# Delta heads: decay matrix and score matrix of a direction side by side in one buffer, both written by one multiply of 128x256

## The chip, the cores and the metric

One core of one Trainium2 chip runs the program. The metric is device time in microseconds (us). The kernel before takes 2635.76 us, the median of 3 runs (2635.53 to 2638.45).

## What is computed

One step of a backbone of two layers with shared code. A layer normalises its input (128 context tokens and 512 latent tokens, width 2048), makes one large input projection and hands its columns to three groups of heads: 8 gated delta heads, 4 attention heads and 4 pooling groups. Each result is multiplied by a gate of its own, all are concatenated and go through one output projection. The change lies in the delta heads:

```
def gated_delta_chunked(q, k, v, g, beta, s0):
    gc = jnp.cumsum(g, axis=-1)
    decay = jnp.exp(jnp.where(tri, gc[..., :, None] - gc[..., None, :], -jnp.inf))
    kb = k * beta[..., None]
    lmat = jnp.where(strict, jnp.einsum('nbhid,nbhjd->nbhij', kb, k) * decay, 0.0)
    rhs = jnp.concatenate([kb * jnp.exp(gc)[..., None], v * beta[..., None]], axis=-1)
    sol = lax.linalg.triangular_solve(lmat + eye, rhs, left_side=True, lower=True, unit_diagonal=True)
    w, u = sol[..., :DK], sol[..., DK:]
    attn = jnp.einsum('nbhid,nbhjd->nbhij', q, k) * decay
...
    def step(s, xs):
        v_new = u_i - jnp.einsum('bhcd,bhde->bhce', w_i, s)
        o = jnp.einsum('bhcd,bhde->bhce', qg_i, s) + jnp.einsum('bhij,bhje->bhie', attn_i, v_new)
        s = s * gl_i[..., None, None] + jnp.einsum('bhcd,bhce->bhde', kg_i, v_new)
```

It is run forwards and backwards over the tokens, with decays and betas of their own for each direction. What matters: `lmat` and `attn` are two products of the same keys (with keys and with queries), multiplied by the same decay matrix and by the same beta (the kernel puts the beta of `v_new` into `attn`).

## The kernel before, in words

**Order of the work.** The program is recorded as a list of operations in program order, and a planner (class `Sched`) then sets for each engine the order in which its instructions are issued. It simulates the program with a cost per instruction; whenever an engine is free it takes the ready operation that stands first in the program. A tile is given a place when its first operation is planned; a tag has a fixed number of places, and an operation whose tile finds none is put off until an older tile of the tag is dead. So the number and the lifetimes of the tiles of a tag decide the order on all engines. On the chip each engine issues its instructions in the planned order and waits by semaphores. All instructions are issued from one line, L499, so in the trace one tells them apart by tiles and shapes.

**Memory.** `memory()` lays the tags into regions: the slab S, the rounded slab R (operands of the large projections, `slabr` in the rows), and two regions W and V (`slabW`, `slabV`), each used for several things in turn. While the delta heads run, W holds four decay matrices `E` of 128x640 (two directions of two heads), two `qg` and `dj`; V holds four score matrices `At` of 128x640, two `ktok` and `cd`. The weights of the next layer's modulation, `ad2w`, lie over the start of W in two buffers.

**A head.** `delta(l, h, ins)` takes the transposed keys, queries and values of 5 chunks of 128 tokens. For each direction a row of cumulated decays is loaded from DRAM to all 128 partitions (a decay matrix, 320 KB), a mask is added, and five exponentials are taken. `to_tok` transposes the keys on TensorE. Then comes the score loop (L1234 to L1247): for a chunk, keys and queries are split into a rounded part and a rest, three products on TensorE give 128x256 in PSUM (keys by keys in the first 128 columns, keys by queries in the others), and four VectorE multiplies of 128x128 make `At` and then `E` of each direction, the latter in place.

After it the diagonal 32x32 blocks go through DRAM into 40 partitions, VectorE solves them in 31 steps of two instructions (`40xN` in the rows: a product and a sum), a `40x1024` copy transposes the result, and it goes back through DRAM. Block products on TensorE (32x32, then 64x64), which read `E`, build the inverse `XT`. Then comes the recurrence, 5 steps in both directions, whose products with `At` read the score matrix up to the last step. A normalisation of 128x5 instructions follows, the transposes, the multiplication into the gate tile `sza`, and the store of `sza`.

**What runs beside it.** `phase_a` calls `delta(h)` and then `head_in(h + 1)`, which makes the projections (products `psum<-slabr`) and convolutions of the next head, so the projections of head h+1 are the work that TensorE has beside head h. After the last head come four pooling groups:

```
        for h in range(H):
            self.delta(l, h, nxt)
            if h + 1 < H:
                nxt = self.head_in(l, h + 1)
        for g in range(4):
            self.pool_group(l, g)
            if l == 0:
                self.ada_cols(l + 1, 16 + 4 * g, 20 + 4 * g, "ad2w", "pr2", 2)
```

A pooling group has one projection for its input and one in `silu_gate`, for which it needs a place of `sza` (there are three) and banks of the PSUM tag `acc` (three); its output product is `psum<-slab,slabV` with 128x128 and 128x512. `ada_cols` loads `ad2w` and multiplies with it.

Of the kernel before, what the change touches and what calls it, by code (L numbers as in the profile page):

```python
# [13 lines left out]
ALU = mybir.AluOpType  # L14
# [9 lines left out]
NT = 5  # L24
# [19 lines left out]
WW = {"W": 4096, "V": 4480}  # L44
# [4 lines left out]
def toff(t):  # L49
    return 0 if t == 0 else 2 + 128 * t  # L50
# [451 lines left out]
class Body:  # L502
# [5 lines left out]
    def memory(self):  # L508
        tags = self.nc.tags

        def put(space, o, specs, top, rounded=False):
            for name, n, w in specs:
                self.nc.tag(name, space, w, [o + i * w for i in range(n)], rounded)
                o += n * w
            assert o <= top, (specs[-1], o, top)
            return o

        at = lambda name: tags[name].slots[0]
# [6 lines left out]
        put("V", 0, [("kpl", 1, 768), ("qps", 1, 640), ("qnh", 1, 640), ("qnl", 1, 640), ("knh", 1, 768), ("knl", 1, 768), ("wkl", 1, 256)], WW["V"], True)  # L525
        put("V", 0, [("cqh", 1, 1920), ("cql", 1, 1920)], WW["V"], True)
        put("W", 0, [("wrh", 1, 768), ("wrl", 1, 768), ("wqh", 2, 384), ("wql", 2, 384)], WW["W"], True)
        put("W", 0, [("E", 4, 640), ("qg", 2, 640), ("dj", 1, 128)], WW["W"])
        put("V", 0, [("At", 4, 640), ("ktok", 2, 640), ("cd", 1, 320)], WW["V"])
        put("W", at("E"), [("ad2w", 2, 2048)], WW["W"])  # L530
        put("V", at("cd"), [("wg", 1, 128)], WW["V"])
        fix = put("S", 0, [("cs", 1, 960), ("ones", 1, 128), ("cw", 1, 240), ("misc", 1, 20), ("dtb", 1, 32), ("nega", 1, 32),
                           ("bn", 1, 96), ("ccol", 1, 64), ("acl", 2, 32), ("bcl", 2, 32), ("mcol", 4, 32), ("raw", 2, 1024)]
# [4 lines left out]
        c = tags["q"].slots + tags["vT"].slots + tags["k"].slots  # L538
# [23 lines left out]
        t = self.nc.tag  # L562
# [620 lines left out]
    def delta(self, l, h, ins):  # L1183
        nc, a = self.nc, self.a
        v = nc.vector
        kT, qT, vT, sza = ins
        ident = self.ident
        E = []
        for d in range(2):
            e = self.T("E", [128, NT, 128])  # L1190
            nc.sync.dma_start(e.rearrange("p t c -> p (t c)"), self.gcd[0].rearrange("(d h t) c -> d h (t c)", d=2, h=8)[d, h].partition_broadcast(128))
            v.tensor_tensor(e, e, self.mask[d].unsqueeze(1).to_broadcast([128, NT, 128]), op=ALU.add)
            for t in range(NT):
                nc.scalar.activation(e[:, t], e[:, t], AF.Exp, bias=self.NGC[:, d * 8 + h, t:t + 1])
            E.append(e)
        ktok = self.T("ktok", [128, NT, 128])
# [3 lines left out]
        bneg, kgs = self.T("bneg", [128, 2, NT]), self.T("kgs", [128, 2, NT])  # L1200
# [29 lines left out]
        v.tensor_tensor(iz, rs, rs, op=ALU.mult)  # L1230
        v.scalar_tensor_tensor(bneg, iz.unsqueeze(1).to_broadcast([128, 2, NT]), -1.0, dh(self.BT), op0=ALU.mult, op1=ALU.mult)
        v.tensor_tensor(kgs, bneg, dh(self.EKG), op=ALU.mult)
        At = [self.T("At", [128, NT, 128]) for _ in range(2)]
        for t in range(NT):  # L1234
            p = self.ps("pr")
            o = toff(t)
            hi, lo = (self.T("kq", [128, 256], F32R) for _ in range(2))
            for i, x in enumerate((kT, qT)):
                c = slice(128 * i, 128 * i + 128)
                self.copy(hi[:, c], x[:, o:o + 128])  # L1240
                self.rest(lo[:, c], x[:, o:o + 128], hi[:, c])
            nc.tensor.matmul(p[:, 0:256], hi[:, 0:128], hi, start=True, stop=False)
            nc.tensor.matmul(p[:, 0:256], hi[:, 0:128], lo, start=False, stop=False)
            nc.tensor.matmul(p[:, 0:256], lo[:, 0:128], hi, start=False, stop=True)
            for d in range(2):
                v.scalar_tensor_tensor(At[d][:, t], p[:, 128:256], bneg[:, d, t:t + 1], E[d][:, t], op0=ALU.mult, op1=ALU.mult)
                v.scalar_tensor_tensor(E[d][:, t], p[:, 0:128], bneg[:, d, t:t + 1], E[d][:, t], op0=ALU.mult, op1=ALU.mult)  # L1247
        M = E
        cd = self.T("cd", [128, 10, 32])
        for b in range(4):  # L1250
# [29 lines left out]
        qg = []  # L1280
# [77 lines left out]
        for step in range(NT):  # L1358
            for d in range(2):
                t = 0 if step == 0 else (step if d == 0 else 5 - step)  # L1360
# [51 lines left out]
        for g0, g1 in ((0, 4), (4, 5)):  # L1412
            p = self.ps("o")
# [253 lines left out]
```

## Time and profile before

| what | value |
|---|---|
| time, median of 3 runs | 2635.76 us (2635.53 to 2638.45) |
| the profiled execution: time, span | 2642.71 us, 2640.6 us |
| mean granted clock of TensorE | 0.982 |
| ScalarE, GpSimd busy | 1026.8 us (39%), 739.7 us (28%) |
| moved over HBM | 313.07 MB read, 31.46 MB written |
| chain that ended last | TensorE 80%, DMA 6%, VectorE 3%, ScalarE 2%, GpSimd 1% |

PE is TensorE's matmuls, PEld its weight loads (which overlap the matmuls), DVE VectorE, ACT ScalarE, POOL GpSimd, SP the engine that issues the DMAs. Of two layers, the delta heads run from about 495 to 1060 us in the first and from about 1790 to 2350 us in the second. The granted clock is given as a share of full speed. Two levels occur, 1.2 and 2.4 GHz, so 0.50 is the lower one and a value between is a mean over a stretch.

### The profile page before, as it was taken

How to read it: one execution, taken by the hardware profiler on the slowest of the kernel's cores; microseconds unless marked ns; L12 is line 12 of the kernel's file. 1: busy time of each engine (PE TensorE's matmuls, PEld its weight loads, DVE VectorE, ACT ScalarE, POOL GpSimd, SP SyncE). 2: the span in 40 equal slices, each digit the busy share in tenths (PEclk: the TensorE clock that was granted, in tenths of full speed). 3: DMA queues.
4: the chain of work that ended last, by engine and by line, in shares of the span. 5: the costliest groups of instructions: out<-in, count | busy, mean ns of one | idle time of the engine just before them, and what ended most of it. 6: DMA issues, size and time to landing. Idle time of an engine off the chain costs nothing.

```text
span 2640.6 us, 52982 instructions
## 1 busy us (share of the span) xinstructions
PE 2541.0 (96%) x20553; PEld 2380.4 (90%) x20553; DVE 1664.4 (63%) x4229; ACT 1026.8 (39%) x2789; POOL 739.7 (28%) x825
## 2 busy tenths in 40 slices
PE   4999999999999999999988999999999999999998
PEld 1689999999999998878888999999999999988888
DVE  3545556888888886332257365678878887755225
ACT  3233345444444432222247333444444444323222
POOL 0021112354333333220025211233444333334002
PEclk7999999999999999999998999999999999999999
DMA  9944444332343333896755434523433334336225
GB/s 314 335 108 110 133 116 121 96 95 83 92 103 101 102 91 100 235 271 173 190 182 157 126 95 126 149 78 91 101 103 90 91 92 103 84 84 194 92 75 191
DMA packets 541202, 347.98 MB, mean 132 GB/s; under 512 B 103826, under 2 KB 499734, under 8 KB 540310
## 3 DMA queue, kind: packets, MB, share of 16 engines
q1 hardware_dynamic: 540950, 344.59, 46.7%
q8 instruction: 162, 2.65, 0.4%
q14 instruction: 90, 0.74, 0.1%
HBM read 313.07 MB, written 31.46 MB: 130 GB/s over the span
## 4 chain that ended last, share of the span: by engine, by line
PE 80%; DMA 6%; DVE 3%; ACT 2%; POOL 1%; issue 1%; SPq 1%; DVEq 0%; ACTq 0%
PE psum L499 80%; DVE slab L499 3%; DMA slab<-d 2%; DMA slab<-in_w_in_dram 1%; DMA slab<-in_w_ada_dram 1%; ACT slab L499 1%; POOL slabr L499 1%; DMA slabW<-in_w_ada_dram 1%; DMA d<-slab 1%; SPq L499 1%; ACT slabr L499 1%; ACT slabW L499 0%; DMA slab<-in_x_sample_dram 0%; DVE slabV L499 0%; DMA slabW<-d 0%
## 5 line engine op out<-in xcount | busy, mean ns | idle before, releaser
L499 PE MATMUL psum<-slabr 128*128 128x384 f32 (+2 forms) x11760 | 2011.1, 324 | 2.3 <-DVE slabW L499 1.0
L499 PEld LDWEIGHTS psum<-slabr 128*128 128x128 f32 x11760 | 1778.2, 190 | 86.9 <-issue 23.5
L499 POOL TENSOR_TENSOR slabr<-slab,slabr 128x512 fp32r<-128x512 f32 (+3 forms) x428 | 482.8, 1136 | 1200.3 <-ACT slabr L499 878.8
L499 ACT ACTIVATE slabr<-slab 128x512 fp32r<-128x512 f32 (+3 forms) x731 | 393.3, 548 | 879.2 <-PE psum L499 726.5
L499 DVE TENSOR_TENSOR slabr<-slab,slabr 128x512 fp32r<-128x512 f32 (+3 forms) x404 | 262.8, 654 | 416.1 <-ACT slabr L499 363.8
L499 PE MATMUL psum<-slab 128*128 128x128 f32 (+4 forms) x4375 | 434.7, 256 | 56.7 <-DVE slab L499 31.9
L499 DVE TENSOR_TENSOR slab<-slab 128x5 f32<-128x5 f32 (+20 forms) x1298 | 473.2, 376 | 19.2 <-DMA slab<-d 3.9
L499 ACT ACTIVATE slab<-psum 128x128 f32<-128x128 f32 (+6 forms) x823 | 276.1, 351 | 492.5 <-PE psum L499 384.7
L499 PEld LDWEIGHTS psum<-slab 128*128 128x128 f32 (+4 forms) x4375 | 352.1, 140 | 97.5 <-DVE slab L499 39.3
L499 DVE SCALAR_TENSOR_TENSOR slab<-slab 128x5 f32<-128x5 f32 (+7 forms) x618 | 348.2, 572 | 42.9 <-ACT slab L499 33.9
L499 ACT ACTIVATE slab<-slab 128x642 f32<-128x642 f32 (+4 forms) x240 | 141.1, 603 | 62.3 <-DVE slab L499 55.7
L499 DVE COPY slab<-psum 32x160 f32<-32x160 f32 (+9 forms) x214 | 84.0, 399 | 112.7 <-PE psum L499 98.0
L499 DVE TENSOR_SCALAR slab<-slab 128x1 f32<-128x1 f32 (+7 forms) x363 | 111.4, 326 | 29.0 <-ACT slabW L499 16.2
L499 POOL TENSOR_SCALAR slab<-slabV,slab 128x128 f32<-128x128 f32 x128 | 58.1, 460 | 217.5 <-PE psum L499 216.9
L499 DVE SCALAR_TENSOR_TENSOR slab<-psum,slab 128x128 f32<-128x128 f32 (+1 forms) x216 | 80.1, 378 | 56.4 <-PE psum L499 54.5
L499 DVE TENSOR_REDUCE slab<-psum 128x4 f32<-128x16 f32 (+3 forms) x104 | 39.5, 380 | 106.5 <-PE psum L499 105.3
L499 PE MATMUL psum<-slab,slabW 32*32 32x32 f32 (+2 forms) x1216 | 80.8, 219 | 14.5 <-DMA slab<-d 7.8
L499 POOL TENSOR_TENSOR slab<-slab 128x640 f32<-128x640 f32 (+5 forms) x46 | 68.1, 1481 | 95.1 <-ACT slab L499 77.8
L499 ACT ACTIVATE slab<-psum,slab 128x256 f32<-128x256 f32 (+2 forms) x93 | 58.7, 641 | 78.3 <-DVE slab L499 74.6
L499 PEld LDWEIGHTS psum<-slab,slabW 32*32 32x32 f32 (+2 forms) x1216 | 66.3, 132 | 23.1 <-DMA slab<-d 10.7
L499 DVE SCALAR_TENSOR_TENSOR slab<-slab,psum 128x128 f32<-128x128 f32 (+2 forms) x160 | 62.0, 395 | 37.2 <-PE psum L499 25.9
L499 PE MATMUL psum<-slab,slabV 128*128 128x128 f32 (+1 forms) x352 | 72.4, 296 | 1.9 <-DVE slab L499 1.4
(61 smaller groups left out, 1384.5 us busy)
## 6 DMA issues: line engine op xcount, KB each, us to landing
slab<-in_w_in_dram SPq DMA_DIRECT2D x186, 512.0 KB
slab<-in_w_ada_dram SPq DMA_DIRECT2D x32, 1024.0 KB
slabW<-in_w_ada_dram SPq DMA_DIRECT2D x32, 1024.0 KB
slab<-in_w_out_dram SPq DMA_DIRECT2D x64, 512.0 KB
slabW<-d SPq DMA_DIRECT2D x64, 320.0 KB
slabV<-in_w_ada_dram SPq DMA_DIRECT2D x32, 512.0 KB
slabW<-in_w_ada_dram SPq DMA_DIRECT2D x32, 512.0 KB
d<-slab SPq DMA_DIRECT2D x32, 320.0 KB
```

The costliest lines, as they stand in the source:

```text
L499: op.inst = getattr(getattr(nc, op.eng), op.meth)(*[real(x) for x in op.a], **{n: real(x) for n, x in op.k.items()})
```

## The change

A direction's decay matrix and score matrix now lie in one buffer of 128 x 5 x 2 x 128, `EA0` in W for the forward direction and `EA1` in V for the backward one, two buffers each. For each chunk the score matrix has the first 128 columns and the decay matrix the next. Queries and keys change places in the split, so that PSUM holds the products in the same order, and one multiply of 128x256, with the decay matrix read twice, writes both. The reload of a decay matrix writes 5 runs of 128 elements per partition instead of one of 640. `ad2w` lies over `EA0`.

```diff
--- before.py
+++ after.py
@@ -525,9 +525,9 @@
         put("V", 0, [("kpl", 1, 768), ("qps", 1, 640), ("qnh", 1, 640), ("qnl", 1, 640), ("knh", 1, 768), ("knl", 1, 768), ("wkl", 1, 256)], WW["V"], True)
         put("V", 0, [("cqh", 1, 1920), ("cql", 1, 1920)], WW["V"], True)
         put("W", 0, [("wrh", 1, 768), ("wrl", 1, 768), ("wqh", 2, 384), ("wql", 2, 384)], WW["W"], True)
-        put("W", 0, [("E", 4, 640), ("qg", 2, 640), ("dj", 1, 128)], WW["W"])
-        put("V", 0, [("At", 4, 640), ("ktok", 2, 640), ("cd", 1, 320)], WW["V"])
-        put("W", at("E"), [("ad2w", 2, 2048)], WW["W"])
+        put("W", 0, [("EA0", 2, 1280), ("qg", 2, 640), ("dj", 1, 128)], WW["W"])
+        put("V", 0, [("EA1", 2, 1280), ("ktok", 2, 640), ("cd", 1, 320)], WW["V"])
+        put("W", at("EA0"), [("ad2w", 2, 2048)], WW["W"])
         put("V", at("cd"), [("wg", 1, 128)], WW["V"])
         fix = put("S", 0, [("cs", 1, 960), ("ones", 1, 128), ("cw", 1, 240), ("misc", 1, 20), ("dtb", 1, 32), ("nega", 1, 32),
                            ("bn", 1, 96), ("ccol", 1, 64), ("acl", 2, 32), ("bcl", 2, 32), ("mcol", 4, 32), ("raw", 2, 1024)]
@@ -1185,10 +1185,13 @@
         v = nc.vector
         kT, qT, vT, sza = ins
         ident = self.ident
-        E = []
+        E, At, EA = [], [], []
         for d in range(2):
-            e = self.T("E", [128, NT, 128])
-            nc.sync.dma_start(e.rearrange("p t c -> p (t c)"), self.gcd[0].rearrange("(d h t) c -> d h (t c)", d=2, h=8)[d, h].partition_broadcast(128))
+            ea = self.T(f"EA{d}", [128, NT, 2, 128])
+            At.append(ea[:, :, 0])
+            e = ea[:, :, 1]
+            EA.append(ea)
+            nc.sync.dma_start(e, self.gcd[0].rearrange("(d h t) c -> d h t c", d=2, h=8)[d, h].partition_broadcast(128))
             v.tensor_tensor(e, e, self.mask[d].unsqueeze(1).to_broadcast([128, NT, 128]), op=ALU.add)
             for t in range(NT):
                 nc.scalar.activation(e[:, t], e[:, t], AF.Exp, bias=self.NGC[:, d * 8 + h, t:t + 1])
@@ -1230,21 +1233,19 @@
         v.tensor_tensor(iz, rs, rs, op=ALU.mult)
         v.scalar_tensor_tensor(bneg, iz.unsqueeze(1).to_broadcast([128, 2, NT]), -1.0, dh(self.BT), op0=ALU.mult, op1=ALU.mult)
         v.tensor_tensor(kgs, bneg, dh(self.EKG), op=ALU.mult)
-        At = [self.T("At", [128, NT, 128]) for _ in range(2)]
         for t in range(NT):
             p = self.ps("pr")
             o = toff(t)
             hi, lo = (self.T("kq", [128, 256], F32R) for _ in range(2))
-            for i, x in enumerate((kT, qT)):
+            for i, x in enumerate((qT, kT)):
                 c = slice(128 * i, 128 * i + 128)
                 self.copy(hi[:, c], x[:, o:o + 128])
                 self.rest(lo[:, c], x[:, o:o + 128], hi[:, c])
-            nc.tensor.matmul(p[:, 0:256], hi[:, 0:128], hi, start=True, stop=False)
-            nc.tensor.matmul(p[:, 0:256], hi[:, 0:128], lo, start=False, stop=False)
-            nc.tensor.matmul(p[:, 0:256], lo[:, 0:128], hi, start=False, stop=True)
+            nc.tensor.matmul(p[:, 0:256], hi[:, 128:256], hi, start=True, stop=False)
+            nc.tensor.matmul(p[:, 0:256], hi[:, 128:256], lo, start=False, stop=False)
+            nc.tensor.matmul(p[:, 0:256], lo[:, 128:256], hi, start=False, stop=True)
             for d in range(2):
-                v.scalar_tensor_tensor(At[d][:, t], p[:, 128:256], bneg[:, d, t:t + 1], E[d][:, t], op0=ALU.mult, op1=ALU.mult)
-                v.scalar_tensor_tensor(E[d][:, t], p[:, 0:128], bneg[:, d, t:t + 1], E[d][:, t], op0=ALU.mult, op1=ALU.mult)
+                v.scalar_tensor_tensor(EA[d][:, t], p[:, 0:256].rearrange("p (i c) -> p i c", i=2), bneg[:, d, t:t + 1], E[d][:, t].unsqueeze(1).to_broadcast([128, 2, 128]), op0=ALU.mult, op1=ALU.mult)
         M = E
         cd = self.T("cd", [128, 10, 32])
         for b in range(4):
```

The planner makes a new order from it. Three places are shown.

TensorE, at the end of the heads of layer 0 (`slabr` is an operand of a projection; `slabW` and `slabV` are the regions W and V; `slab` is everything else; 128x512 with `slabV` is a pooling product). Before:

```order
L499 MATMUL psum<-slabr 128x384 x7
L499 MATMUL psum<-slab,slabV_3862 128x128
L499 MATMUL psum<-slabr 128x384 x28
L499 MATMUL psum<-slab,slabV_3862 128x512
L499 MATMUL psum<-slab 128x128 x4
L499 MATMUL psum<-slab,slabV_3862 128x128
L499 MATMUL psum<-slab 128x128
L499 MATMUL psum<-slab,slabW_3582 128x128
L499 MATMUL psum<-slabr 128x256 x5
L499 MATMUL psum<-slab,slabV_3862 128x512
L499 MATMUL psum<-slabr 128x256 x31
```

Now, the end of a run of 19 rows that hold no projection:

```order
L499 MATMUL psum<-slab,slabW_3582 128x128 x2
L499 MATMUL psum<-slab 128x128
L499 MATMUL psum<-slab,slabV_3587 128x128
L499 MATMUL psum<-slab 128x128
L499 MATMUL psum<-slab,slabW_3582 128x128
L499 MATMUL psum<-slab 128x128 x4
L499 MATMUL psum<-slab,slabW_3582 128x128 x2
L499 MATMUL psum<-slab,slabV_3587 128x128
L499 MATMUL psum<-slab 128x128 x5
L499 MATMUL psum<-slab,slabV_3587 128x128
L499 MATMUL psum<-slab,slabV_3587 128x512
L499 MATMUL psum<-slab,slabW_3582 32x32 x10
```

Before, the first pooling product is followed by head 6's four transposes and then by projections; now it stands behind the recurrence of head 6 and is followed at once by the first block products of head 7.

VectorE, the same place (`40xN` are steps of head 7's inverse, `128x5` the normalisation of head 6, `slab<-psum,slab 128x128` and `slab<-slab,psum 128x128` its recurrence). Before:

```order
L499 COPY slab<-psum 128x512
L499 TENSOR_TENSOR slab<-slab 40x192
L499 SCALAR_TENSOR_TENSOR slab<-slab 128x5
L499 TENSOR_TENSOR slab<-slab 40x8x24
L499 TENSOR_SCALAR slab<-slab 128x5
L499 TENSOR_TENSOR slab<-slab 40x175
L499 TENSOR_SCALAR slab<-slab 128x5
L499 TENSOR_TENSOR slab<-slab 40x7x25
```

Now:

```order
L499 SCALAR_TENSOR_TENSOR slab<-slab,psum 128x128 x2
L499 TENSOR_TENSOR slab<-slab 40x175
L499 TENSOR_TENSOR slab<-slab 40x7x25
L499 TENSOR_TENSOR slab<-slab 40x156
L499 SCALAR_TENSOR_TENSOR slab<-psum,slab 128x128
L499 TENSOR_TENSOR slab<-slab 40x6x26
L499 SCALAR_TENSOR_TENSOR slab<-psum,slab 128x128
L499 TENSOR_TENSOR slab<-slab 40x135
```

At the same step of head 7's inverse, head 6 was in its normalisation and is now in its recurrence.

SP, the DMAs around the reload of head 2 in layer 0 (`d_1398` holds the cumulated decays and their exponentials; `out_dram` 128x128 are head 0's final states; a load of `d_4839` or `d_4824` into 40x1024 is the way into the inverse of head 1). Before:

```order
L499 DMA d_4839<-slabV_3862 128x10x32
L499 DMA slabW_3582<-d_1398 128x640
L499 DMA slab<-in_w_in_dram 128x8x128
L499 DMA slabW_3582<-d_1398 128x640
L499 DMA slab<-d_4839 40x1024
L499 DMA out_dram<-slab 128x128 x2
L499 DMA slab<-in_w_in_dram 128x8x128 x2
L499 DMA slab<-in_state_delta_fwd_dram 128x128
L499 DMA slab<-in_state_delta_bwd_dram 128x128
L499 DMA slabW_3582<-d_1398 128x640 x2
```

Now:

```order
L499 DMA d_4824<-slabV_3587 128x10x32
L499 DMA slab<-d_4824 40x1024
L499 DMA slab<-in_w_in_dram 128x8x128
L499 DMA out_dram<-slab 128x128 x2
L499 DMA slab<-in_w_in_dram 128x8x128 x2
L499 DMA slabW_3582<-d_1398 128x640
L499 DMA slab<-in_state_delta_fwd_dram 128x128
L499 DMA slab<-in_state_delta_bwd_dram 128x128
L499 DMA slabW_3582<-d_1398 128x5x128
L499 DMA slabW_3582<-d_1398 128x640
L499 DMA slabV_3587<-d_1398 128x5x128
```

The two decay matrices of head 2 (now 128x5x128) stood ahead of the inverse's load and of head 0's outputs, and now stand behind them and behind three loads of projection weights.

## Rows read from the trace of the kernel before

**Rows 1.** The page, part 1: busy us, share of the span, instructions.

```profile
PE 2541.0 (96%) x20553; PEld 2380.4 (90%) x20553; DVE 1664.4 (63%) x4229; ACT 1026.8 (39%) x2789; POOL 739.7 (28%) x825
```

**Rows 2.** Windows: length, then busy PE, PEld, DVE, ACT, POOL, clock, DMA share, GB/s.

```profile
528.00:1023.00 495.00, 488.24 (x4120) 479.06 (x4119) 405.65 (x1077) 216.76 (x665) 197.48 (x221) 1.00 0.37 94
1821.00:2277.00 456.00, 450.18 (x3731) 442.79 (x3730) 375.87 (x994) 205.76 (x635) 185.99 (x205) 0.99 0.36 95
```

**Rows 3.** Waits of PE, 495 to 1023 us: total us, times, longest.

```profile
PE psum L499 <- DVE slabW L499: 0.5, 1, 0.5
```

**Rows 4.** Timeline, 1031 to 1058 us: start, length, instruction; idle before and releaser bracketed.

```profile
1031.40 1.02 PE L499 MATMUL psum<-slab,slabV 128*128 128x512 f32 x2
...
1034.03 0.70 PE L499 MATMUL psum<-slab 128*128 128x128 f32 x4 [1.61 <-DVE slab L499]
...
1036.57 1.03 DVE L499 COPY slab<-slab 40x1024 f32<-40x1024 f32 x1
...
1037.45 0.76 ACT L499 ACTIVATE slab<-psum 128x384 f32<-128x384 f32 x2 [3.10 <-DMA d<-slab]
...
1038.58 1.43 PE L499 MATMUL psum<-slabr 128*128 128x256 f32 x5
...
1045.92 0.73 PE L499 MATMUL psum<-slab,slabW 32*32 32x32 f32 x40
...
1046.57 1.49 PE L499 MATMUL psum<-slabr 128*128 128x384 f32 x7
...
1049.50 2.17 PE L499 MATMUL psum<-slabr 128*128 128x384 f32 x14
...
1051.61 1.20 PE L499 MATMUL psum<-slab,slabW 64*64 64x64 f32 x20
```

**Rows 5.** Windows at the end of the heads, columns as in group 2.

```profile
1036.00:1038.00 2.00, 0.64 (x2) 0.35 (x3) 1.70 (x6) 0.55 (x2) 0.00 (x0) 0.50 0.63 209
1030.00:1042.00 12.00, 8.24 (x31) 5.43 (x30) 9.05 (x36) 1.46 (x4) 0.94 (x4) 0.73 0.35 98
2327.00:2339.00 12.00, 8.41 (x31) 5.72 (x30) 8.58 (x34) 1.46 (x4) 0.28 (x4) 0.74 0.35 99
```

**Rows 6.** VectorE's groups by form: count, busy us, mean ns, idle before, releaser.

```profile
L499 DVE SCALAR_TENSOR_TENSOR slab<-psum,slab 128x128 f32<-128x128 f32 x192 | 62.2, 331 | 39.9 <-PE psum L499 38.0
L499 DVE SCALAR_TENSOR_TENSOR slabV<-psum,slab,slabW 128x128 f32<-128x128 f32 x160 | 49.2, 340 | 4.6 <-PE psum L499 4.6
L499 DVE SCALAR_TENSOR_TENSOR slabW<-psum,slab,slabW 128x128 f32<-128x128 f32 x160 | 48.7, 338 | 0.0
...
L499 DVE TENSOR_TENSOR slab<-slab 40x220 f32<-40x220 f32 x64 | 27.6, 431 | 0.6
...
L499 DVE COPY slab<-slab 40x1024 f32<-40x1024 f32 x16 | 22.0, 1375 | 0.1
...
L499 DVE TENSOR_TENSOR slab<-slab 40x135 f32<-40x135 f32 x64 | 18.6, 290 | 1.0
...
L499 DVE SCALAR_TENSOR_TENSOR slab<-slab,psum 128x384 f32<-128x384 f32 x32 | 17.5, 548 | 9.0 <-ACT slab L499 8.8
...
L499 DVE SCALAR_TENSOR_TENSOR slab<-slab,psum 128x256 f32<-128x256 f32 x32 | 13.1, 410 | 0.9 <-ACT slab L499 0.9
```

**Rows 7.** Chain that ended last: start us, length us, what.

```profile
597.02 4.17 DMA slabW<-d
...
745.09 4.31 DMA slab<-in_w_in_dram
```

**Rows 8.** Timeline of PE in layer 1's recurrence, columns as in group 4.

```profile
2365.54 0.38 PE L499 MATMUL psum<-slab 128*128 128x128 f32 x2
2365.76 0.39 PE L499 MATMUL psum<-slab,slabV 128*128 128x128 f32 x2
```

**Rows 9.** Waits of PE, 1060 to 1200 us, columns as in group 3.

```profile
PE psum L499 <- DMA slabW<-in_w_ada_dram: 4.6, 4, 2.3
```

**Rows 10.** Chain at the end of layer 0's heads.

```profile
1023.81 12.30 DVE slab L499 x37
```

## The prediction

> **What bounds the kernel now.** I read the page first: TensorE is busy for 96% of the span and VectorE for 63% [rows 1]. A share over the whole span says nothing about the stage that is changed, so next come the two stretches in which the heads follow each other, one per layer: there TensorE is busy for 488.24 of 495 us and for 450.18 of 456 us, at a granted clock of 1.00 and 0.99, with VectorE busy for 82% of both [rows 2]. So 12.6 us of idle TensorE are all that a faster head could win there, and the list of waits gives 0.5 us of the first stretch to VectorE's writes into W, where half of the changed multiplies go [rows 3]. The score stage of a head is hidden by the projections of the next one.
>
> The cover ends once per layer, at the end of the heads. There the projections of the pooling groups are the only other work, and the third group stops half way: its second PSUM bank stays taken until an older gate is read out, which waits for a gate tile that is free only once head 6 is stored. The rows show that: after the pooling product at 1031.40 TensorE waits for VectorE, ScalarE's gate evacuation at 1037.45 waits 3.10 us for the store, and the projections go on at 1038.58 [rows 4]. The granted clock is 0.50 (1.2 GHz) at 1036 to 1038 us, behind these microseconds with little work [rows 5]. In the 12 us around it TensorE has 8.24 us of busy time and a mean clock of 0.73, and the same in layer 1 [rows 5]. That is the stretch to watch.
>
> **The change, part by part.**
>
> *The multiply.* 320 instructions of 128x128, at 340 and 338 ns, become 160 of 128x256 [rows 6]. No row has this very form; the nearest are an instruction of 128x256 at 410 ns and one of 128x384 at 548 ns, each with one operand in PSUM [rows 6]. I take 440 ns, just above the row of the same size, because here one operand is read twice. VectorE goes from 97.9 us to 160 x 0.44 = 70.4 us, 27.5 us less (by the bounds 32 to 10 us less). On the path that sets the end: nothing, since TensorE waits 0.5 us for these writes in a whole stretch [rows 3]; if that cover were gone, 1.7 us per head. The 256 columns are the same three products with q and k exchanged: nothing.
>
> *The strided reload.* A decay matrix was loaded in runs of 2560 B, and now in runs of 512 B. The projection weights already arrive in runs of 512 B, 512 KB in 4.31 us, where a decay matrix of 320 KB took 4.17 us [rows 7]. So the load stays near 4 us: bounds 0 and 0.3 us, taken as 0. The mask, the exponentials and the block copies read rows 256 apart instead of 128, with the same runs of 128: 0.
>
> *Where the buffers live and when they come free.* A decay matrix was free after the last block product with it, before its head's recurrence. Now it shares a buffer with the score matrix, which the last step of the recurrence still reads. Two buffers per direction stay, so head h+2 can reload only after head h has ended. The SyncE rows show it: the reload of head 2 stands behind the outputs of head 0 and three projection loads instead of ahead of them. What hides this is the distance to the multiply: in the steady stretch a reload of 4.2 us, a mask and ten exponentials fit beside the previous head. I price it at 0 on TensorE. If that cover is gone it is one reload per head on the head's own chain, which TensorE sees only where it has no projections left.
>
> *The order at the end of the heads.* This is where the sum is made. In the order before, head 6 ends its recurrence under the projections, and what lies bare is its normalisation between the inverse of head 7. In the changed order head 6 is later, and the projections run out in the middle of its recurrence: 19 rows of TensorE, from the third step to the pooling product, have no projection among them. The bare stretch now has three pieces.
>
> 1. The rest of the recurrence, on VectorE between the inverse of head 7: 19 steps of the inverse, whose groups lie between 290 and 431 ns (mean about 0.355: 6.7 us), 8 of its other multiplies at 0.33 (2.6 us) and the copy at 1.4 us [rows 6], together 10.7 us. TensorE has 20 products in it at 0.22 us each, from start to start [rows 8], 4.4 us. Dry: 6.3 us.
> 2. From the end of that copy to the first block product of head 7, which waits for the inverse to go to DRAM and back: 1037.60 to 1045.92, 8.3 us, in the trace [rows 4]. There projections cover it; now TensorE has 12 products of 0.22 us and one 128x512 of 1.0 us [rows 4], 3.6 us. Dry: 4.7 us, less the two multiplies that still follow the copy (0.7 us): 4.0 us.
> 3. The block products of head 7 up to the first 64x64 ones: 1045.92 to 1052.81, 6.9 us, in the trace, with 21 projections (3.7 us) among them [rows 4]. Bare I take 5 us with the other 3.2 us of work. Dry: 1.8 us.
>
> Together 12.1 us dry per layer. The stretch that it replaces has between 3.8 us (12 minus 8.24 us of products) and 6.6 us (12 minus 5.43 us of weight loads) [rows 5]; I take 6.6, since a lone product's busy time holds its own latency. So +5.5 us per layer. The bounds are +8.3, with 3.8 us, and 0, if pieces 2 and 3 lie inside piece 1 and nothing but its 6.3 us is dry. The clock took 12 x 0.27 = 3.2 us per layer before [rows 5]. The new stretch is twice as long but a little over half filled: its clock costs at least the same, and at most 4 us more, if all of its 11 us of work (4.4, 3.6 and 3.2) ran at half speed and so took 11 us longer, of which the 12 us dry hide most. I take the same.
>
> *The gate weights of layer 1.* Their two buffers lie over the decay buffers in W, so in layer 0 the first load now waits for the end of head 7 instead of its block products, about 100 products later. TensorE already waits 4.6 us for these loads [rows 9]. Bounds 0 and twice that; since the first is then used 36 products after its issue instead of 40, I take 0.
>
> **Sum.** 2 x 5.5 = +11 us on the profiled execution, 2642.7 to 2653.7 us. That execution lies 6.95 us above the median of the runs (2642.71 against 2635.76), so in terms of the median: 2646.8, say 2646 us, 0.4% slower. A measurement of this kernel can tell about 0.2% from no change, 5.3 us.
>
> **The rivals.**
>
> *Faster: the shorter multiply arrives.* Each head's chain is about 1.7 us shorter, and if head 6 gets through its recurrence before the projections run out, the bare stretch shrinks: its present price is 6.6 + 3.2 us per layer. Four tenths of that gone in both layers give 2635.8 - 8 = 2628 us. It decides from the point where head 6 is some 5 us earlier than the changed order has it. Against it: VectorE also has the inverse of head 7 between, and the reload now waits for head 4. The Trainium skill (VectorE: DVE Perf Modes, Rules for kernel authors) tells authors to minimise the number of VectorE instructions, and would expect this side; the trace agrees on the instruction (410 ns for twice the columns), not yet on the span. Chance 0.13.
>
> *No change: the two ends cancel.* In the new order the normalisation of head 6 no longer has the inverse between its small steps, which took 1023.81 to 1036.1 us [rows 10]; if pieces 2 and 3 overlap with it better than I reckon, the new stretch is about as dry as the old one: 2636 us. Chance 0.22.
>
> *Slower still.* The half filled stretch drops to 1.2 GHz early (+4 us per layer) and the gate weights wait twice as long (+4.6 us): 2646 + 12.6 = 2659 us. The rows have the clock at 0.50 after a few microseconds with little work [rows 5]. The Trainium skill (TensorE: Matmul & The Clock Gate, Why this matters for your kernels) warns that idle gaps between matmul bursts throw the engine back to its lower clock; the trace agrees, at 0.50 here. Chance 0.18.
>
> That the change does not do what it says would be a multiply of 128x256 as slow as two of 128x128, 678 ns; the row of 128x384 at 548 ns rules it out [rows 6].
>
> **How the numbers follow.** The forecast, 2641 to 2652 us, has 0.47, and with the slower rival 0.65 lie above 2641. No change has 0.22, faster 0.13. The range goes from 2635, which takes in most of no change, to 2660, with the slower rival; left out are the faster side and what lies above, about 0.2.
>
> **What would show it.** VectorE busy 25 to 30 us less; a group of 160 multiplies of 128x256 near 440 ns; the stretches where the heads follow each other as full as now; at the end of the heads a bare stretch of some 23 us in place of 7, with TensorE waiting for VectorE and for the loads from DRAM, and a granted clock under 1 for at least as long. I am wrong if TensorE's idle time there does not grow, if the steady stretches open gaps at the mask (a late reload), or if the time moves with VectorE's.

## The result, and the profile after

The changed kernel takes 2660.97 us, the median of 4 runs (2659.87 to 2662.72), beside 2635.65 us of the kernel before: a ratio of 1.0094 with an interval of 1.0077 to 1.0112. It is 25 us slower, more than twice the 11 us of the forecast, and a microsecond above the range.

The page, part 1 of the changed kernel (busy us, share of the span, instructions), answers to [rows 1]. TensorE has as many instructions as before, and is busy 11.6 us longer.

```profile
span 2659.7 us, 52763 instructions
PE 2552.6 (96%) x20553; PEld 2387.0 (90%) x20553; DVE 1650.1 (62%) x4054; ACT 1017.0 (38%) x2792; POOL 756.9 (28%) x837
```

VectorE's groups by form: the wide multiply has two groups, one per region. It takes 474 ns on average where the two that it replaces took 678 [rows 6]: 75.8 us in place of 97.9, so 22.1 us less.

```profile
L499 DVE SCALAR_TENSOR_TENSOR slabW<-psum,slab,slabW 128x256 f32<-128x256 f32 x80 | 38.1, 477 | 11.6 <-PE psum L499 11.3
L499 DVE SCALAR_TENSOR_TENSOR slabV<-psum,slab,slabV 128x256 f32<-128x256 f32 x80 | 37.7, 471 | 0.0
```

VectorE as a whole is busy only 14.3 us less, where 25 to 30 were forecast. The planner sets more than the order: for some operations it also chooses the engine, and in the new plan 12 instructions of 128x642 that ScalarE had (94 before, 82 now) are VectorE's. First before, then after:

```profile
L499 DVE TENSOR_SCALAR slab<-slab 128x642 f32<-128x642 f32 x2 | 1.1, 548 | 0.0
L499 DVE TENSOR_SCALAR slab<-slab 128x642 f32<-128x642 f32 x14 | 12.9, 921 | 5.3 <-ACT slab L499 5.0
```

Windows over the stretches in which the heads follow each other (columns as in group 2). They are fuller than before [rows 2]: 2.8 us of TensorE idle in 472, 3.5 in 469. The loss is not here.

```profile
528.00:1000.00 472.00, 469.18 (x3874) 461.57 (x3872) 378.20 (x941) 207.16 (x651) 206.06 (x216) 1.00 0.38 97
1821.00:2290.00 469.00, 465.46 (x3856) 457.49 (x3855) 372.19 (x940) 206.60 (x653) 201.82 (x214) 0.99 0.36 94
```

It is at the end of the heads. The timeline of TensorE there, layer 0:

```profile
1023.96 0.95 PE L499 MATMUL psum<-slabr 128*128 128x384 f32 x4
...
1033.35 1.22 PE L499 MATMUL psum<-slab 128*128 128x128 f32 x5 [1.01 <-DVE slab L499]
...
1038.81 0.48 PE L499 MATMUL psum<-slab 128*128 128x128 f32 x1 [2.90 <-ACT slabW L499]
...
1040.98 2.08 PE L499 MATMUL psum<-slab,slabV 128*128 128x512 f32 x2 [0.44 <-DVE slab L499]
1043.15 0.59 PE L499 MATMUL psum<-slab,slabW 32*32 32x32 f32 x14
...
1050.19 1.01 PE L499 MATMUL psum<-slab,slabW 64*64 64x64 f32 x7
...
1054.30 0.78 PE L499 MATMUL psum<-slabr 128*128 128x256 f32 x2
```

The last projection (`slabr`) starts at about 1024.6 us and the next at 1054.30. Before, the last one started at 1031.2 and the next at 1038.58 [rows 4], 7.4 us later. I call the time from the start of one projection to the start of the next the **bare stretch**: 29.7 us now, and 30.7 us in layer 1. Windows over the two, same columns: the granted clock is 0.73 and 0.71.

```profile
1024.60:1054.30 29.70, 21.95 (x193) 15.66 (x192) 18.93 (x64) 7.86 (x35) 9.61 (x17) 0.73 0.28 78
2329.60:2360.30 30.70, 21.75 (x193) 15.67 (x192) 21.15 (x64) 7.80 (x35) 9.62 (x17) 0.71 0.27 76
```

The 128x512 product (two records) took 2.08 us there, at a granted clock of 0.50, and 1.02 us before [rows 4]. The waits of TensorE in the first of these stretches:

```profile
PE psum L499 <- DVE slab L499: 3.8, 7, 1.0
PE psum L499 <- ACT slabW L499: 3.4, 2, 2.9
PE psum L499 <- ACT slab L499: 0.3, 1, 0.3
```

### The profile page after: what moved, and what is told of

The parts are those of the page before. It is cut to its first block, busy times and chain, and to the rows that moved or that the text cites. A ratio compares the mean times of both kernels' runs of the same rounds, so it can differ in the third digit from the quotient of the medians.

```text
span 2659.7 us, 52763 instructions
## 1 busy us (share of the span) xinstructions
PE 2552.6 (96%) x20553; PEld 2387.0 (90%) x20553; DVE 1650.1 (62%) x4054; ACT 1017.0 (38%) x2792; POOL 756.9 (28%) x837
## 4 chain that ended last, share of the span: by engine, by line
PE 78%; DMA 8%; DVE 5%; ACT 1%; SPq 1%; issue 1%; POOL 0%; DVEq 0%; ACTq 0%
PE psum L499 78%; DVE slab L499 5%; DMA slab<-d 2%; DMA slabW<-in_w_ada_dram 2%; DMA slab<-in_w_ada_dram 1%; DMA slab<-in_w_in_dram 1%; DMA d<-slab 1%; SPq L499 1%; ACT slab L499 1%; DMA slabV<-d 0%; DVE slabV L499 0%; ACT slabW L499 0%; POOL slabr L499 0%; DMA slab<-in_x_sample_dram 0%; ACT slabr L499 0%
## 5 line engine op out<-in xcount | busy, mean ns | idle before, releaser
L499 PE MATMUL psum<-slabr 128*128 128x256 f32 (+2 forms) x11760 | 1998.8, 323 | 0.9 <-ACT slabr L499 0.9
L499 POOL TENSOR_TENSOR slabr<-slab,slabr 128x512 fp32r<-128x512 f32 (+3 forms) x440 | 496.1, 1136 | 1245.2 <-ACT slabr L499 954.1
L499 ACT ACTIVATE slab<-psum 128x128 f32<-128x128 f32 (+7 forms) x823 | 276.5, 352 | 601.8 <-PE psum L499 502.1
L499 DVE TENSOR_TENSOR slab<-slab 128x5 f32<-128x5 f32 (+21 forms) x1298 | 475.7, 376 | 35.6 <-DMA slab<-d 12.2
L499 DVE SCALAR_TENSOR_TENSOR slab<-slab 128x5 f32<-128x5 f32 (+8 forms) x618 | 345.4, 570 | 47.7 <-ACT slab L499 42.7
L499 ACT ACTIVATE slab<-slab 128x642 f32<-128x642 f32 (+4 forms) x228 | 132.3, 596 | 54.5 <-DVE slab L499 49.5
L499 DVE TENSOR_SCALAR slab<-slab 128x1 f32<-128x1 f32 (+8 forms) x375 | 125.9, 355 | 33.8 <-ACT slabW L499 15.3
L499 PE MATMUL psum<-slab,slabW 128*128 128x128 f32 (+2 forms) x896 | 101.8, 242 | 10.8 <-DMA slab<-d 9.8
L499 PEld LDWEIGHTS psum<-slab,slabW 128*128 128x128 f32 (+2 forms) x896 | 82.8, 156 | 23.8 <-DMA slab<-d 14.2
L499 PE MATMUL psum<-slab,slabV 32*32 32x32 f32 (+3 forms) x672 | 69.9, 245 | 3.3 <-DVE slab L499 2.4
```

The source lines that it names most:

```text
L499: op.inst = getattr(getattr(nc, op.eng), op.meth)(*[real(x) for x in op.a], **{n: real(x) for n, x in op.k.items()})
```

## The experiments

Every ratio is against the kernel before, run beside it, whose median was 2636.42 us for the first four runs, 2640.74 for the next four, and 2639.61 for the last four. Three theories stood at first. **L**: the longer lifetime of the decay matrix makes the bare stretch. **S**: the strided loads or the shared buffer cost. **M**: the wide multiply costs. Each kernel has a plan of its own, of order and engines, unless the text says otherwise.

**1. The decay matrices held, nothing else.** The kernel before; in the planner's books the last product with `At` also holds `E`.

```diff
-                    nc.tensor.matmul(pt, At[d][:, t], Zt, start=False, stop=(nmm == 14))
+                    last = nc.tensor.matmul(pt, At[d][:, t], Zt, start=False, stop=(nmm == 14))
+                    if step == NT - 1:
+                        E[d].t.left += 1
+                        E[d].t.ops.append(last)
+                        last.tiles.append(E[d].t)
```

> Theory L (lifetimes): the loss comes from the decay matrix being held until the last step of its head's recurrence; head h+2 starts later, the projections run out inside head 6's recurrence, and the bare stretch that follows runs at the lower clock. Then holding the decay matrices of the kernel before, with its separate buffers, contiguous loads and four 128x128 multiplies, loses most of it: 2650 to 2662 us, and a stretch of 15 to 20 us at 1.2 GHz at the end of the heads in both layers. Theory S (strided access): the loads in runs of 512 B and the wider buffer cost; this kernel has neither: 2636 us. Theory M (the wide multiply or the order that follows from its length): 2636 us too.

Measured: 2649.73 us, ratio 1.0054 (1.0040 to 1.0067). In this plan the longer lifetime costs 13 to 14 us, a little over half of the loss, with no strided load and no wide multiply. The bare stretch is 12.8 us in both layers; the clock is at 1.2 GHz for 10.2 us in each, less than the 15 to 20 forecast.

**2. Merged buffers, two multiplies.** The change, with the multiply written as two of 128x128.

```diff
-                v.scalar_tensor_tensor(EA[d][:, t], p[:, 0:256].rearrange("p (i c) -> p i c", i=2), ...
+                v.scalar_tensor_tensor(At[d][:, t], p[:, 0:128], bneg[:, d, t:t + 1], E[d][:, t], ...
+                v.scalar_tensor_tensor(E[d][:, t], p[:, 128:256], bneg[:, d, t:t + 1], E[d][:, t], ...
```

> The merged buffers with two 128x128 multiplies per direction and chunk. Theory L: as the kernel with held decay matrices, within 3 us, 2650 to 2662 us, with VectorE busy some 25 us more than with the one multiply. Theory S: slower than the held kernel by what the change cost, so 2655 to 2661 us beside 2636 there. Theory M: back to 2636 us, since the wide multiply is gone.

Measured: 2647.02 us, 1.0044 (1.0031 to 1.0057), and 12.8 and 12.7 us bare. As the held kernel: S falls, and the strided loads cost nothing that can be measured between these two plans. But theory L explains only half, and the other half goes with the multiply or with the plan made for it.

**3. One multiply, lifetimes apart.** `E` and `At` of a direction are tiles of their own with places 640 columns apart, and the multiply writes across both.

```diff
-        put("W", 0, [("EA0", 2, 1280), ("qg", 2, 640), ("dj", 1, 128)], WW["W"])
-        put("V", 0, [("EA1", 2, 1280), ("ktok", 2, 640), ("cd", 1, 320)], WW["V"])
+        for i, sp in enumerate("WV"):
+            self.nc.tag(f"At{i}", sp, 640, [0, 1280])
+            self.nc.tag(f"E{i}", sp, 640, [640, 1920])
...
-                v.scalar_tensor_tensor(EA[d][:, t], p[:, 0:256].rearrange("p (i c) -> p i c", i=2), ...
+                v.scalar_tensor_tensor(Pair(At[d], E[d], t), p[:, 0:256].rearrange("p (i c) -> p i c", i=2), ...
```

> The one multiply of 128x256 is kept, but decay matrix and score matrix are tiles of their own that lie 640 columns apart, so the decay matrix is free after the last block product and is reloaded contiguously. Theory L: the loss is gone, 2628 to 2638 us, and the stretch at 1.2 GHz at the end of the heads is back to 7 us or less. Theory S: gone as well, 2630 to 2638 us. Theory M: the loss stays, 2655 to 2661 us.

Measured: 2641.17 us, 1.0016 (1.0006 to 1.0026). M falls: the wide multiply is there and most of the loss is gone. The bare stretch is 6.6 us, shorter than before, yet the kernel is not faster than before.

**4. The kernel before, once more.**

> The kernel before once more, for a second profile. The profiled execution of before took 2642.7 us, 7 us above the median of the runs; its trace has three drops of the clock in the stretches where the heads follow each other. If those drops differ from execution to execution, this one shows others or none and takes 2635 to 2643 us with the same 7 us of lower clock at the end of the heads.

Measured: 2641.08 us in one run. Drops of the clock in the steady stretches do differ from execution to execution: this profile has one at 2125 us, where the first had 1.00, and none at 681 and 2203 us, where the first had them. Two executions of one kernel so differ by some microseconds, and a term is better read from stretches than from spans. At the end of the heads the bare stretch is 7.2 and 7.3 us again, with the clock at 1.2 GHz for 6.8 and 3.4 us.

Now theory **O** was added: the other half comes from the plan that the planner makes when it reckons with the shorter multiply. Runs 5 to 7 put each kind of multiply into each order.

**5. The change beside them.** No edit.

> The change itself, beside the other kernels of this call on one chip. It measured 25 us over the kernel before, while the held kernel and the one with merged buffers and two multiplies lose only 11 to 13 us. All theories: 2655 to 2663 us here too; if it comes out near 2648 us instead, half of the loss belonged to the earlier occasion and not to the kernel.

Measured: 2661.67 us, 1.0087 (1.0073 to 1.0101), bare stretches of 30.2 and 29.9 us. The loss belongs to the kernel.

**6. The order of the change, two multiplies issued.** When the order has been made, each wide multiply is issued as its two halves.

```diff
-            op.inst = getattr(getattr(nc, op.eng), op.meth)(*[real(x) for x in op.a], ...
+            for a, k in op.halves:
+                op.inst = getattr(getattr(nc, op.eng), op.meth)(*[real(x) for x in a], ...
```

> The order of the change, instruction by instruction on every engine, but each wide multiply is issued as two of 128x128 at its place. Theory O (the second half of the loss comes from the order that the planner makes with the shorter multiply, in which head 6 is later still): as the change, 2655 to 2663 us. Theory M (the wide multiply itself costs): back to the kernel with two multiplies, 2645 to 2650 us.

Measured: 2673.5 us, 1.0135 (1.0116 to 1.0153): 12 us slower than the change, where neither theory had it. In this order the wide multiply is a gain. The bare stretch is 30.0 and 30.1 us, as in run 5, so the 12 us lie elsewhere. In the profile (the slowest of the four runs) TensorE is idle for 6.1 and 8.1 us where the heads follow each other, against 3.4 and 4.3 us in run 5, most of it in waits for the loads of the inverse. The clock is at 1.2 GHz there for 6.8 and 17 us, and in run 5 not at all; such falls vary between executions. Windows of run 6, then of run 5, columns as in group 2:

```profile
528.00:1000.00 472.00, 465.93 (x3821) 456.03 (x3820) 389.98 (x1001) 205.39 (x646) 202.99 (x216) 0.99 0.37 94
1821.00:2290.00 469.00, 460.90 (x3866) 449.84 (x3867) 377.57 (x965) 204.60 (x648) 196.68 (x207) 0.98 0.37 94
```

```profile
528.00:1000.00 472.00, 468.60 (x3871) 461.00 (x3871) 378.93 (x943) 207.93 (x653) 205.17 (x217) 1.00 0.37 96
1821.00:2290.00 469.00, 464.68 (x3868) 456.56 (x3866) 376.84 (x945) 207.35 (x655) 202.64 (x215) 1.00 0.37 94
```

**7. The order of run 2, one multiply issued.** The same edit the other way: the first half issues nothing, the second the wide multiply.

> The order of the kernel with merged buffers and two multiplies, but each pair is issued as one multiply of 128x256 at the place of the second. Theory O: as that kernel or a little less, 2643 to 2649 us. Theory M: as the change, 2655 to 2663 us.

Measured: 2647.1 us, 1.0026 (1.0014 to 1.0038), bare stretch 12.8 us twice. With runs 2 (1.0044), 5 and 6 this makes a square: with either multiply the order of the change is the slower one, by 0.6 to 0.9% of the time, and in either order the wide multiply is no loss (in the older order its intervals overlap with those of two). M is out. O stands, though the 12 us of run 6 were not in its forecast.

**8. Added products in the gaps.** 40 products of 128x128 per layer that nothing reads, planned only where TensorE has nothing else.

```diff
+        if h == H - 1:
+            with nc.later(1000000):
+                for _ in range(40):
+                    op = nc.tensor.matmul(p1[:, 384:512], ident, ident, start=True, stop=True)
...
```

> The change with 40 added products of 128x128 (the identity by itself, into an unused quarter of a PSUM bank) in the gaps of TensorE at the end of the heads of each layer; nothing reads them. Theory C (most of the loss at the end of the heads is TensorE running at 1.2 GHz after the half filled stretch): the stretch at the lower clock shrinks from 17 and 20 us to 7 or less, and the time falls by 8 to 15 us, to 2646 to 2653 us. Theory W (the loss is waiting alone, and work done at the lower clock lies inside the waits): the clock stays up but the time does not fall by more than 3 us, 2657 to 2662 us.

Measured: 2662.23 us, 1.0090 (1.0077 to 1.0103). It told nothing apart: the clock still fell, to 0.50 for 14 and 17 us, only later, when the block products came. The bare stretch is 27.5 and 29.1 us, with TensorE idle for 2.3 and 2.9 us of it. Run 12 adds products further on.

**9. The change with one number altered.** The planner's cost of the wide multiply.

```diff
+        if meth == "scalar_tensor_tensor" and onps and n == 256 and len(a[0].shape) == 3:
+            return 0.36
```

> The change with one number altered: the planner reckons 0.36 us for the wide multiply instead of 0.40. Every instruction is the same, the merged buffers and their lifetimes too; only the order on the engines differs, and the longest run of products without a projection falls from 101 (recurrence of head 6 to block products of head 7) to 59. Theory O (the order at the end of the heads decides): 10 to 20 us less than the change, 2640 to 2652 us. Theory B (the merged buffer costs by itself, whatever the order): within 5 us of the change, 2656 to 2666 us.

Measured: 2647.58 us, 1.0031 (1.0020 to 1.0043), bare stretches of 14.1 and 15.0 us. The same operations in the same merged buffers, and 14 us less. The expectation has every instruction the same, which is not quite so: the planner also chose other engines for some, and the 12 of 128x642 are ScalarE's again. B falls, and O is shown on the change itself, if the plan is taken as a whole, with order and engines.

**10. The same for run 3**, with `return 0.47`.

> The kernel with one multiply and lifetimes apart (2641 us), with the planner reckoning 0.47 us for the multiply, which is what it took on the chip (473 ns), instead of 0.40. Theory O: with no long run of products without projections (34 at most) and earlier heads it is at or below the kernel before, 2625 to 2638 us. If the truer number does not help: 2640 to 2648 us.

Measured: 2644.9 us, 1.0018 (1.0007 to 1.0028). The bare stretch is down to 4.2 us, and the time is not: theory O's 2625 to 2638 us did not come. Beyond some point it is no longer this stretch that decides. VectorE has ten of the instructions of 128x642 here (14 in the change), so their place alone does not make the loss; no run holds the engines fixed and alters the order alone. What keeps runs 3 and 10 some 4 to 5 us above before was not found.

**11. The kernel before with one number altered**, 0.34 for each of its score multiplies (tags `E` and `At`, 128 columns).

> The kernel before, its instructions, buffers and lifetimes unchanged, with the planner reckoning 0.34 us for each of the score multiplies, as measured, instead of 0.26. Theory O says that such a number alone moves the time through the order, by as much as the change did in part: off the 2636 to 2640 us of before by more than 5 us, and slower, since the heads are planned later: 2643 to 2660 us. If the order of before is robust against it: 2633 to 2641 us.

Measured: 2656.55 us, 1.0066 (1.0054 to 1.0079). Not an operation or a buffer differs from the kernel before, and it loses 17 us; the bare stretch is 16.5 us. The plan does differ, in the engines too: GpSimd has 861 instructions against 825, and VectorE 42 fewer. The truer number gave the worse order.

**12. Added products through the whole stretch.** As run 8, with 44 in place of 40, and 17 more per layer around the block products of head 7, which take their PSUM bank earlier. The planner makes a new plan around them.

```diff
+        keep(p2, 384, 4)
         T1 = self.T("T1", [128, NT, 32])
...
+        keep(rc[0], 0, 6)
         p4 = self.ps("lv")
...
+        keep(rc[0], 0, 4)
         T2 = self.T("T2", [128, NT, 64])
...
+        keep(rc[0], 0, 3)
```

> The change with added products that nothing reads, as in the earlier fill, and now also among the block products of head 7, so that TensorE has wide products through the whole stretch at the end of the heads. Theory C (the lower clock costs some 6 us per layer): the stretch at 1.2 GHz falls from 17 to 20 us to 7 or less, and the time to 2645 to 2655 us. Theory W (the chain waits for VectorE and the DMAs, whatever the clock): the clock stays up and the time stays, 2657 to 2665 us.

Measured: 2657.62 us, 1.0071 (1.0058 to 1.0084). The clock stays at 1.00 through both bare stretches, which shrink to 26.1 us, and the time is 0.16% below that of run 5, with overlapping intervals. The time is in W's range and not in C's. But the run does not give the clock's price. The added products stand ahead of useful ones, and the first block product comes 22.0 us after the last projection, against 19.2 in run 5; from there to the end of the first 64x64 products it takes 6.6 us against 9.1. The stretch ends earlier also because projections now stand ahead of the 64x64 products. The 4 us may so be a gain less a loss.

The windows over the first bare stretch, columns as in group 2, first of run 4 (the kernel before):

```profile
1028.00:1035.20 7.20, 3.63 (x14) 1.87 (x13) 6.90 (x29) 1.46 (x4) 0.14 (x2) 0.79 0.25 80
```

of run 1 (held):

```profile
1027.90:1040.70 12.80, 5.60 (x17) 2.72 (x15) 12.50 (x44) 2.75 (x13) 4.55 (x7) 0.69 0.15 47
```

of run 9 (the change at 0.36):

```profile
1031.20:1045.30 14.10, 8.88 (x116) 6.26 (x115) 7.15 (x26) 2.05 (x6) 2.38 (x5) 0.69 0.34 85
```

of run 11 (before at 0.34):

```profile
1030.30:1046.80 16.50, 7.65 (x29) 4.22 (x27) 14.62 (x48) 5.16 (x26) 7.49 (x10) 0.69 0.18 60
```

of run 5 (the change), and of run 12 (filled):

```profile
1026.80:1057.00 30.20, 22.96 (x193) 16.62 (x192) 18.77 (x64) 7.92 (x35) 9.62 (x17) 0.66 0.27 77
```

```profile
1022.40:1048.50 26.10, 25.63 (x294) 24.03 (x292) 16.87 (x59) 7.36 (x34) 9.00 (x17) 1.00 0.31 77
```

Roughly, the time rises with the length of this stretch: ratios of 1 at 7 us, 1.0026 to 1.0054 at 13 to 15 (runs 1, 2, 7 and 9), 1.0066 at 16.5, 1.0087 at 30. It is not the only thing that counts: runs 3 and 10 have 1.0016 and 1.0018 at 6.6 and 4.2 us, and run 6 has 1.0135 at 30. It is not in proportion either; in the longer stretches lie more products that have to be done anyway (193 records in run 5 against 14 in run 4).

## Why the prediction was wrong, point by point

**What bounds the kernel: right.** The steady stretches stayed full, and the longer bare stretch lies where the prediction said to watch. In it TensorE waited for VectorE (3.8 us in layer 0) and ScalarE (3.7 us), but not for loads from DRAM as forecast. The run of products without a projection, from head 6's third step to head 7's block products, is there in both layers.

**The multiply: the price was near, its worth only partly.** 474 ns against 440. "On the path that sets the end: nothing" held in the older order (run 7 beside run 2), but not in the order of the change, where two multiplies cost 12 us more (run 6), mostly where the heads follow each other and so in the stretches that were taken as covered. The sentence that I took from the Trainium skill (VectorE: DVE Perf Modes, Rules for kernel authors), fewer VectorE instructions, agrees with the trace: VectorE is busy 14.3 us less, and in a given order the one multiply is never the slower. It says nothing of the order.

**The strided reload: right** as far as run 2 beside run 1 can tell, two kernels with plans of their own.

**The lifetimes: right in kind**, and worth 11 to 14 us in the plans of runs 1 and 2. It is no fixed price: run 9 has the longer lifetimes too and loses 8 us, and run 11 loses 17 us without them.

**One wait was missed.** The backward decay matrix now lies in V, which by the memory plan the attention heads use until head 0 begins. In the chain its load comes behind TensorE's products. Chain, then ScalarE's and TensorE's timelines of the changed kernel:

```profile
403.38 5.88 DMA slabV<-d
```

```profile
411.10 0.40 ACT L499 ACTIVATE slabV<-slabV,slab 128x128 f32<-128x128 f32 x1 [2.23 <-DVE slabV L499]
...
411.72 0.33 PE L499 MATMUL psum<-slab 128*128 128x128 f32 x1 [1.96 <-ACT slab L499]
```

ScalarE stands in its exponentials for this matrix, a PSUM read for TensorE is queued behind, and TensorE waits 2.0 us (2.4 in layer 1), 4.4 us of the 25. Run 3 has the wait too (1.6 us in layer 0) and run 1 almost not (0.4). I had costed the buffers' places at nothing and had looked at the reloads only, not at the first load.

**The order at the end of the heads: the right term, mis-sized. This is the step that failed**, and with it the clock, taken as unchanged. The three pieces came to 10.7, 8.3 and 5 us, 24 us together; they measured 29.7 in the profiled execution:
- piece 1, up to the end of the 40x1024 copy, at 1032.09 plus 1.03 us: 8.5 us from the last projection, less than the 10.7;
- piece 2, to the first block product at 1043.15: 10.0 us against 8.3. The block products stand behind the pooling product, which took 2.08 us at half clock;
- piece 3, to the end of the first 64x64 products: 9.1 us against 5, and the projections go on only 2.1 us later, at 1054.30. At a clock of 1.00 the same block products took 6.9 us in the kernel before, with 21 projections among them, and 6.6 us in run 12, with added products. So the 5 us were too short by up to 1.6 us at full clock, the lower clock goes with some 2.5 us more, and the stretch had been ended 2.1 us too early.

Windows over piece 3, of the change, of the kernel before and of run 12:

```profile
1043.15:1052.22 9.07, 7.80 (x128) 6.57 (x128) 6.61 (x24) 2.05 (x6) 0.69 (x4) 0.50 0.13 48
```

```profile
1045.92:1052.81 6.89, 6.89 (x143) 6.36 (x142) 2.21 (x6) 1.65 (x5) 0.00 (x0) 1.00 0.80 210
```

```profile
1044.39:1050.97 6.58, 6.31 (x139) 5.40 (x138) 4.90 (x14) 1.89 (x6) 0.20 (x2) 1.00 0.28 109
```

With 29.7 us, 11.2 us of products and 6.6 us replaced, the sum gives 11.9 us per layer, 23.8 us together. The measurement says 25, but that is in part luck: the profiled executions, on which the sum was made, lie 20 us apart (2662.72 and 2642.71), 4.4 us belong to the wait above, and the 29.7 us already hold what the clock cost. By the prediction's own measures, time without weight loads is 14.0 and 15.0 us in the two layers against 12.1, and the clock takes 8.0 and 8.9 us against 3.2: two thirds of the miss would be the clock's. A sum cannot tell the two apart, since products at 1.2 GHz lengthen the stretch.

**The clock: "I take the same" was wrong.** It took 27% of 29.7 us, 8.0 us of full speed per layer, against 3.2. The Trainium skill (TensorE: Matmul & The Clock Gate, Why this matters for your kernels) warns of this fall, and the rows agree: 0.73. What it cost in time stays open. Run 12 gained about 4 us with the clock at 1.00, after its added products had put off the first block product by some 3 us per layer. An estimate from the windows over piece 3, 9.1 against 6.6 us, is 2.5 us per layer for these products alone.

**The gate weights: right.** TensorE waits 3.4 us for them, against 4.6 [rows 9].

**The rivals.** "Slower still", 2659 us, came nearest. Its clock was there, its wait for the gate weights was not, and its two terms made up, by luck, for a bare stretch taken too short. What none of the cases had is that the size of the loss is an accident of the plan: it is 1.0087 with the planner's own number for the multiply and 1.0031 with 0.36.

## What to carry to other kernels

Merging two buffers gives both the longer of the two lifetimes; ask when the shorter one used to be reloaded, and keep them as separate tiles in neighbouring places if one instruction is to write both. Where a planner makes the order, compare a change with the old kernel in several orders (a cost altered by a tenth or a third is enough): one such number moved the change by 14 us down and the kernel before by 17 us up, with the same operations. Check also whether the planner has moved work to another engine. A bare stretch has to be followed to the first product that fills it again, and its products priced at the clock that they will get; what the clock and the waits cost apart from each other was not settled here.

## What the runs showed of the hardware that was not expected

The clock also falls in the middle of the steady stretches, at the block products, after a wait of little more than a microsecond. Windows of run 3, columns as in group 2, and its timeline of TensorE:

```profile
672.00:676.00 4.00, 4.00 (x31) 3.96 (x30) 3.47 (x8) 2.74 (x7) 1.53 (x3) 1.00 0.91 174
676.00:680.00 4.00, 2.47 (x51) 2.11 (x50) 3.45 (x5) 0.74 (x1) 1.19 (x1) 0.93 0.92 174
680.00:684.00 4.00, 4.00 (x68) 3.71 (x68) 1.14 (x5) 0.59 (x2) 0.00 (x0) 0.50 0.31 96
```

```profile
678.09 0.41 PE L519 MATMUL psum<-slab,slabW 32*32 32x32 f32 x14 [1.53 <-DMA slab<-d]
```

TensorE waits 1.53 us for a load and then has 32x32 products, which keep it busy by the profile, and the clock is 0.50 right behind. The second profile of the kernel before has the same at another head, behind a wait of 1.43 us:

```profile
2123.22 0.73 PE L499 MATMUL psum<-slab,slabW 32*32 32x32 f32 x40 [1.43 <-DMA slab<-d]
```

```profile
2125.00:2131.00 6.00, 6.00 (x78) 5.71 (x77) 4.82 (x13) 2.81 (x8) 0.13 (x1) 0.50 0.32 66
```

Most heads have such products without a fall, and which one has it differs from execution to execution. In run 8, too, the clock held as long as the added products ran and fell when the block products came, though TensorE was idle for only 2.3 us of 27.5; in run 12, with more added products among the block products, it did not fall. No run tells the wait from the small products as the reason.
